# Opening loads in smaller parts and in order of use, first norm weights as columns, and a pinned sequence of the opening work in a two-layer decoder trunk

## The chip, the cores and the metric

The kernel runs on one core of a Trainium2 chip. The metric is the time of one execution on the device, in microseconds (us). The engines are TensorE (PE; PEld are its weight loads), VectorE (DVE), ScalarE (ACT), GpSimd (POOL) and SyncE (SP), which here only issues DMAs.

## The reference

Two layers over 256 tokens with 2048 features. Layer 0 mixes tokens with a chunkwise mLSTM, layer 1 with a gated linear recurrence (RG-LRU); each mixer and each SwiGLU feed-forward stands behind an RMS norm and adds to the residual. Only the start of layer 0 bears on the change:

```python
def rms_norm(x, g):
    xf = x.astype(jnp.float32)
    y = xf * lax.rsqrt(jnp.mean(xf * xf, axis=-1, keepdims=True) + EPS)
    return (y * g.astype(jnp.float32)).astype(x.dtype)
...
for layer in range(DEPTH):
    hn = rms_norm(h, norm_mix[layer])
    mix = mlstm_mixer(hn, ...)      # proj = hn @ w_in; q, k, v, o, gates = split(proj); ...
    h = h + mix
    h = h + swiglu(rms_norm(h, norm_ffn[layer]), ffn_w_in[layer], ffn_w_out[layer])
return rms_norm(h, norm_final)
```

## The kernel before

Every matrix product is done in three passes: an operand is split into a high part (a float32r rounding, the cast on ScalarE) and a low part (what is left, a subtraction on VectorE), and the products high by high, high by low and low by high are added up in PSUM.

The weights stream through four rotating buffers. `stream` loads two K tiles (256 rows of 512 columns, 512 KB, named raw0, raw2, ... by the first K tile) with one DMA of the sync queue, ScalarE makes whi (`nc.scalar.copy`, L210) and VectorE wlo (`nc.vector.tensor_tensor`, L211). `linear_feat` uses them: for each of 16 K tiles 12 matmuls of 256 columns (`mm_feat`, L309 to L311: whi by x high, whi by x low, wlo by x high, for four groups of 128 features). The first such product is qk00, the queries of the first four heads; qk01, qk10 and qk11 follow.

Its other operand is x transposed and scaled by the norm's weights, also as high and low parts. `Norm.quarter(q)` makes four K tiles of it: 8 transposes on TensorE into PSUM (L359, tile tr_m), four scalings on ScalarE (L365, the high part) and four on VectorE (L369, the low part). The scale per token, 1/rms, is applied later: `Norm.stats` sums squares of x on ScalarE (L345, eight instructions in all, result scrap into junk), `finish` turns them into factors (VectorE, GpSimd) and spreads them over all partitions with the matmul bc (L403). After it 16 matmuls gp (L545) compute the mLSTM gates from x and the small weight gwx, which is loaded as gw.

x lies in the tile h. `load_x` loads it in four DMAs of 512 columns (512 KB), with the first eight K tiles of weights between them. Norm weights and other per-feature vectors are loaded as rows, up to 128 rows of 128 numbers in each of three tiles, and turned into columns with a transpose (L181, tile par) and a copy on VectorE (`par_cols`, L183). The first rows are those of norm_mix; until par_cols(0) is done, `quarter(0)` has no weights to scale with.

The sequence on each engine is that of a scheduler: it sorts by the place in the program and by what it reckons to be ready; `tc.high_priority` pulls an instruction ahead. A DMA takes one of eight completion counters in turn, and the issuing queue waits until the DMA that had the counter before has landed. Twelve matmuls (L142, tile warm) on constants run before any data are there.

Of the kernel before, what the change touches and what calls it, by code (L numbers as in the profile page):

```python
# [8 lines left out]
F32 = mybir.dt.float32  # L9
F32R = mybir.dt.float32r  # L10
AF = mybir.ActivationFunctionType
# [3 lines left out]
P = 128  # L15
# [3 lines left out]
NK = D // P  # L19
# [5 lines left out]
NB = 512  # L25
EPS = 1e-6
BIG = 1e30
AHEAD = 1000
# [14 lines left out]
def kernel(  # L43
# [38 lines left out]
    def pool_of(key):  # L82
        return pools[key][0]
# [15 lines left out]
    def misc(name):  # L99
        return turned("misc", name) if named else bank("bank", name)  # L100
# [13 lines left out]
    h = const.tile([P, NT, D], F32, name="h")  # L114
    xv = x[0].rearrange("(b p) d -> p b d", p=P)
    raw0 = {}

    def load_raw(w, c0, ncols, kg, step=2):
        raw = pool_of("w").tile([P, 2, NB], F32, tag="raw", name=f"raw{kg}")
        wv = w.rearrange("(k p) n -> p k n", p=P)  # L120
        for i in range(0, 2, step):
            nc.sync.dma_start(raw[:, i:i + step, 0:ncols], wv[:, kg + i:kg + i + step, c0:c0 + ncols])
        return raw

    def load_x():
        for q in range(4):
            nc.sync.dma_start(h[:, :, q * NB:(q + 1) * NB], xv[:, :, q * NB:(q + 1) * NB])
# [13 lines left out]
    for i in range(12):  # L141
# [17 lines left out]
        ("gb", r_gate_b.rearrange("l g (k p) -> (l g k) p", p=P), 32),  # L159
        ("cw", r_conv_w.rearrange("l j (k p) -> (l j k) p", p=P), 64),  # L160
    ]
    par = {}
    rows = [const.tile([P, P], F32, name=f"rows{i}") for i in range(3)]
    cols = [const.tile([P, P], F32, name=f"cols{i}") for i in range(3)]
    part, at, used = 0, 0, [0, 0, 0]
    for name, src, n in par_src:
        if part == 0 and at or at + n > P:
            part, at = part + 1, 0
        nc.sync.dma_start(rows[part][at:at + n, :], src)
        if part == 0:  # L170
            load_x()
        par[name] = cols[part][:, at:at + n]
        at += n
        used[part] = at
    bif = const.tile([H, 2], F32, name="bif")
    nc.sync.dma_start(bif, m_b_if[0].rearrange("(two h) -> h two", h=H))

    def par_cols(i):
        n = used[i]
        pt = misc(f"par{i}")  # L180
        nc.tensor.transpose(pt[:, 0:n], rows[i][0:n, :], ident[0:n, 0:n])  # L181
# [13 lines left out]
    def stream(w, c0, nk, ncols=NB):  # L195

        if named:
            yield from stream4(w, c0, nk)
            return
        wpool = pool_of("w")  # L200
        for kg in range(0, nk, 2):
            first = kg in raw0
            raw = raw0.pop(kg) if first else load_raw(w, c0, ncols, kg)
            hi = wpool.tile([P, 2, NB], F32R, tag="whi", name=f"whi{kg}")
            lo = wpool.tile([P, 2, NB], F32R, tag="wlo", name=f"wlo{kg}")
            step = 1 if first and kg == 0 else 2
            with tc.high_priority(offset=0 if first else AHEAD):
                for i in range(0, 2, step):
                    r = raw[:, i:i + step, 0:ncols]
                    nc.scalar.copy(hi[:, i:i + step, 0:ncols], r)  # L210
                    nc.vector.tensor_tensor(  # L211
                        lo[:, i:i + step, 0:ncols], r, hi[:, i:i + step, 0:ncols].bitcast(F32), op=ALU.subtract
                    )
            for i in range(2):
                yield kg + i, hi[:, i, 0:ncols], lo[:, i, 0:ncols]
# [92 lines left out]
    def mm_feat(o, hi, lo, ah, al, first_in_bank, last):  # L308
        nc.tensor.matmul(o, lhsT=hi, rhs=ah, start=first_in_bank, stop=False, skip_group_check=True)  # L309
        nc.tensor.matmul(o, lhsT=hi, rhs=al, start=False, stop=False, skip_group_check=True)  # L310
        nc.tensor.matmul(o, lhsT=lo, rhs=ah, start=False, stop=last, skip_group_check=True)  # L311

    def linear_feat(w, c0, nk, act, name, after=None):

        ps = [acc(f"{name}_{b}").rearrange("p (f t) -> p f t", f=2) for b in range(2)]
        for k, hi, lo in stream(w, c0, nk):
            ah, al = act(k)
            for f in range(4):
                fs = slice(f * P, (f + 1) * P)
                mm_feat(ps[f // 2][:, f % 2, :], hi[:, fs], lo[:, fs], ah, al,  # L320
                        k == 0 and f % 2 == 0, k == nk - 1)
            if after:
                after(k)
            elif k > 1:
                run_pending()
        return ps


    class Norm:
        lag = 0  # L330
        opening = None

        def open(self):
            if self.opening:
                self.opening()

        def __init__(self, name, gain, bcast=False):
            self.name, self.gain, self.bcast = name, gain, bcast
            self.x = []
            self.ss = small.tile([P, NT, 4], F32, tag="ss", name=f"ss_{name}")  # L340

        def stats(self, q, blocks=range(NT)):
            for b in blocks:
                junk = small.tile([P, NB], F32, tag="junk", name="junk", bufs=1)
                nc.scalar.activation(  # L345
                    junk, h[:, b, q * NB:(q + 1) * NB], AF.Square,
                    accum_out=self.ss[:, b, q:q + 1],
                )

        def quarter(self, q):  # L350
            xt = pool_of("x").tile([P, 4, 2, T], F32R, tag=f"x{q}", name=f"x{q}_{self.name}")
            hi, lo = xt[:, :, 0, :], xt[:, :, 1, :]
            self.x.append(xt)
            for j in range(2):
                pt = misc(f"tr_{self.name}{q}{j}").rearrange("p (f t) -> p f t", f=2)
                for f in range(2):
                    k = 4 * q + 2 * j + f
                    for b in range(NT):
                        nc.tensor.transpose(  # L359
                            pt[:, f, b * P:(b + 1) * P], h[:, b, k * P:(k + 1) * P], ident  # L360
                        )
                for f in range(2):
                    k = 4 * q + 2 * j + f
                    g = self.gain[:, k:k + 1]
                    nc.scalar.activation(hi[:, 2 * j + f, :], pt[:, f, :], AF.Copy, scale=g)  # L365
                for f in range(2):
                    k = 4 * q + 2 * j + f
                    g = self.gain[:, k:k + 1]
                    nc.vector.scalar_tensor_tensor(  # L369
                        out=lo[:, 2 * j + f, :], in0=pt[:, f, :], scalar=g,  # L370
                        in1=hi[:, 2 * j + f, :].bitcast(F32), op0=ALU.mult, op1=ALU.subtract,
                    )

        def parts(self, q):

# [117 lines left out]
    def split_store(dst_hi, dst_lo, src):  # L493

        nc.scalar.copy(dst_hi, src)
        nc.vector.tensor_tensor(dst_lo, src, dst_hi.bitcast(F32), op=ALU.subtract)
# [18 lines left out]


    n0 = Norm("m0", par["g_mix"][:, 0:16], bcast=True)
    n0.quarter(0)
    n1 = NormPairs("f0", par["g_ffn"][:, 0:16])

    def mlstm_mixer():
        mx = open_pool("mx", "mx", 2)
        if True:
            w = m_w_in[0]
# [3 lines left out]
            gw = mx.tile([P, NK, 2 * H], F32, name="gw", bufs=1)  # L528
            nc.sync.dma_start(gw, w.rearrange("(k p) n -> p k n", p=P)[:, :, 6144:6160])
# [12 lines left out]
            n0.finish()  # L542
            gp = misc("gp")[0:4 * H, :]
            for k in range(NK):
                nc.tensor.matmul(  # L545
                    gp, lhsT=gwx[:, k, :, :].rearrange("p s n -> p (s n)"), rhs=n0.act2(k),
                    start=(k == 0), stop=(k == NK - 1),
# [568 lines left out]
```

## Time and profile before

| | |
|---|---|
| median of 3 runs | 2103.68 us (2102.78 to 2103.95) |
| the profiled execution | 2105.72 us, its span 2103.9 us |
| mean granted TensorE clock over the span | 0.997 |
| TensorE busy | 2087.6 us, 99% of the span |
| VectorE, ScalarE busy | 1673.3 us (80%), 1313.5 us (62%) |
| HBM read | 401.84 MB, 192 GB/s over the span |
| first matmul of qk00 / end of the last gp | 10.66 us / 43.34 us |

The span runs from the first to the last instruction of the profiled execution; times in the profile count from its start. Names in the profile lose their numbers: tr_m is each of the transposes' PSUM tiles, x_m the scaled x, raw, whi and wlo the weight buffers, qk the sums of the first products. "Idle" in brackets is how long an engine stood before an instruction, and behind it what released it.

### The profile page before, as it was taken

To read this page: it belongs to the slowest core of one execution; us is meant where nothing else is said; L and a number is where in the kernel's file an instruction comes from. 1 tells how busy PE (TensorE), PEld (TensorE's weight loads), DVE (VectorE), ACT (ScalarE), POOL (GpSimd) and SP (SyncE) were. 2 spreads that over 40 slices of the span, in tenths; PEclk is the share of its full clock that TensorE was granted. 3 is DMA by queue.
4 is the path that set the end of the run, shared out by engine and by line. 5 is a ranking of instruction groups with operands and counts; after the bars stand their busy time and mean duration, and the time that the engine had idled before them with its cause. 6 is when DMAs were issued, how large, how long until landed. Compare 5 with 4: busy or idle time off the path is not lost.

```text
span 2103.9 us, 27554 instructions
## 1 busy us (share of the span) xinstructions
PE 2087.6 (99%) x10544; PEld 1766.2 (84%) x10544; DVE 1673.3 (80%) x1808; ACT 1313.5 (62%) x1580; POOL 43.2 (2%) x62
## 2 busy tenths in 40 slices
PE   9999999999999999999999999999999999999998
PEld 8988888877888888888889999788888888888886
DVE  6655556699898988998876786869988898898985
ACT  5444445556676666677664758645666666666764
POOL 0001110000000000000000000000000000000002
PEclk9999999999999999999999999999999999999999
DMA  7555656556665566566555666655666565566653
GB/s 215 163 168 172 180 180 223 187 183 215 202 211 181 197 205 206 201 215 197 168 181 159 192 191 188 223 190 180 211 207 222 182 200 199 182 219 219 201 170 130
DMA packets 211085, 405.75 MB, mean 193 GB/s; under 512 B 14520, under 2 KB 14728, under 8 KB 210824
## 3 DMA queue, kind: packets, MB, share of 16 engines
q1 hardware_dynamic: 210808, 402.94, 59.6%
q8 instruction: 82, 1.34, 0.3%
q10 hardware_dynamic: 144, 1.05, 0.1%
q14 instruction: 51, 0.42, 0.1%
HBM read 401.84 MB, written 2.10 MB: 192 GB/s over the span
## 4 chain that ended last, share of the span: by engine, by line
PE 96%; ACT 2%; DVE 1%; issue 1%; DMA 0%; SPq 0%; ACTq 0%; POOLq 0%; POOL 0%; DVEq 0%
PE P L753 8%; PE P L754 8%; PE P L755 8%; PE out L753 8%; PE out L754 7%; PE out L755 7%; PE Q L753 6%; PE Q L754 6%; PE Q L755 6%; PE po L293 2%; PE po L292 2%; PE po L294 2%; PE qk L309 1%; PE qk L310 1%; PE qk L311 1%; PE v L292 1%
## 5 line engine op out<-in xcount | busy, mean ns | idle before, releaser
L211 DVE TENSOR_TENSOR wlo<-raw,whi 128x1024 fp32r<-128x1024 f32 (+1 forms) x225 | 273.1, 1218 | 183.6 <-ACT whi L210 182.5
L210 ACT CAST whi<-raw 128x1024 fp32r<-128x1024 f32 (+1 forms) x225 | 234.6, 1047 | 206.2 <-PE po L294 44.1
L236 DVE TENSOR_TENSOR wlot<-sum,whit 128x1024 fp32r<-128x1024 f32 x208 | 249.3, 1219 | 72.0 <-ACT whit L235 72.0
L753 PE MATMUL out<-whio,hh 128*128 128x512 f32 x704 | 274.9, 391 | 0.3 <-ACT out L856 0.3
L754 PE MATMUL out<-wloo,hh 128*128 128x512 f32 x704 | 274.4, 390 | 0.4 <-DVE wloo L236 0.4
L755 PE MATMUL out<-whio,hh 128*128 128x512 f32 x704 | 274.0, 390 | 0.0
L235 ACT CAST whit<-sum 128x1024 fp32r<-128x1024 f32 x208 | 213.7, 1051 | 93.7 <-PE Q L755 30.1
L235 ACT CAST whio<-rawo 128x1024 fp32r<-128x1024 f32 (+1 forms) x166 | 183.4, 1106 | 106.8 <-PE out L755 93.8
L236 DVE TENSOR_TENSOR wloo<-rawo,whio 128x1024 fp32r<-128x1024 f32 (+1 forms) x166 | 212.5, 1284 | 11.2 <-ACT whio L235 10.0
L863 ACT COPY h<-out 128x512 f32<-128x512 f32 x154 | 90.2, 586 | 186.4 <-PE out L755 186.3
L236 DVE TENSOR_TENSOR wlox<-raw,whix 128x1536 fp32r<-128x1536 f32 x104 | 182.4, 1754 | 22.4 <-ACT whix L235 22.1
L236 DVE TENSOR_TENSOR wlo<-raw,whi 128x2048 fp32r<-128x2048 f32 x72 | 164.2, 2287 | 23.4 <-ACT whi L235 23.3
L235 ACT CAST whi<-raw 128x2048 fp32r<-128x2048 f32 x72 | 137.0, 1915 | 40.5 <-DMA raw<-in_ffn_w_in_dram 26.2
L235 ACT CAST whix<-raw 128x1536 fp32r<-128x1536 f32 x104 | 154.2, 1483 | 10.6 <-PE P L755 7.6
L753 PEld LDWEIGHTS out<-whio,hh 128*128 128x128 f32 x704 | 132.2, 188 | 29.2 <-ACT out L856 1.4
L754 PEld LDWEIGHTS out<-wloo,hh 128*128 128x128 f32 x704 | 132.2, 188 | 28.5 <-DVE wloo L236 1.2
L755 PEld LDWEIGHTS out<-whio,hh 128*128 128x128 f32 x704 | 132.2, 188 | 27.8
L276 DVE TENSOR_TENSOR sum<-raw 128x1024 f32<-128x1024 f32 x104 | 127.1, 1222 | 5.0 <-DMA raw<-in_ffn_w_in_dram 3.0
L755 PE MATMUL P<-whi,p_f 128*128 128x512 f32 x282 | 110.0, 390 | 0.0
L753 PE MATMUL Q<-whi,p_f 128*128 128x512 f32 x276 | 109.7, 398 | 0.2 <-DVE h L485 0.2
L753 PE MATMUL P<-whi,p_f 128*128 128x512 f32 x282 | 109.7, 389 | 0.0
L754 PE MATMUL P<-wlo,p_f 128*128 128x512 f32 x282 | 109.7, 389 | 0.0
(284 smaller groups left out, 4995.2 us busy)
## 6 DMA issues: line engine op xcount, KB each, us to landing
raw<-in_ffn_w_in_dram SPq DMA_DIRECT2D x352, 512.0 KB, 4.7
rawo<-in_ffn_w_out_dram SPq DMA_DIRECT2D x176, 512.0 KB, 4.3
raw<-in_m_w_in_dram SPq DMA_DIRECT2D x95, 512.0 KB, 3.8
raw<-in_r_w_in_dram SPq DMA_DIRECT2D x64, 512.0 KB, 3.9
raw<-in_m_w_out_dram SPq DMA_DIRECT2D x32, 512.0 KB, 4.0
raw<-in_r_w_out_dram SPq DMA_DIRECT2D x32, 512.0 KB, 3.7
gr<-in_r_gate_w_dram SPq DMA_DIRECT2D x8, 512.0 KB, 3.8
h<-in_x_dram SPq DMA_DIRECT2D x4, 512.0 KB, 7.4
```

The costliest lines, as they stand in the source:

```text
L210: nc.scalar.copy(hi[:, i:i + step, 0:ncols], r)
L211: nc.vector.tensor_tensor(lo[:, i:i + step, 0:ncols], r, hi[:, i:i + step, 0:ncols].bitcast(F32), op=ALU.subtract)
L235: nc.scalar.copy(hi, src)
L236: nc.vector.tensor_tensor(lo, src, hi.bitcast(F32), op=ALU.subtract)
L276: nc.vector.tensor_tensor(t[:, 0:2, :], raw[:, 1:3, :], raw[:, 3:4, :].broadcast_to([P, 2, NB]), op=ALU.add)
L292: nc.tensor.matmul(o, lhsT=ah[:, bs], rhs=hi, start=(k == 0), stop=False)
L293: nc.tensor.matmul(o, lhsT=ah[:, bs], rhs=lo, start=False, stop=False)
L294: nc.tensor.matmul(o, lhsT=al[:, bs], rhs=hi, start=False, stop=(k == nk - 1))
L753: nc.tensor.matmul(o, lhsT=a[0], rhs=b[0], start=start, stop=False, **kw)
L754: nc.tensor.matmul(o, lhsT=a[0], rhs=b[1], start=False, stop=False, **kw)
L755: nc.tensor.matmul(o, lhsT=a[1], rhs=b[0], start=False, stop=stop, **kw)
L863: nc.scalar.copy(hs, o)
```

## The change

`load_x` issues x in parts of 2, 2, 4, 4 and 4 K tiles (256, 256 and three times 512 KB) and the weights of K tiles 0 to 3 in four parts of 256 KB, in the sequence of their use. The first four columns of norm weights come by a DMA of their own, issued by ScalarE, straight as columns (`gain0`: 128 partitions by 4 numbers, 4 bytes at a time), and scale quarter 0; the rows of norm_mix are issued by ScalarE as well, behind its table load. `after(...)` adds edges that pin instructions behind others on the same engine: the first weight casts behind the scalings of x, quarters 1, 2 and 3 of x behind K tiles 1, 5 and 9 (before: program places behind 3, 7 and 11, which the scheduler moved), the rows' transposes, the gate weights' split and the sums of squares further back. Sums of squares write their scrap into the PSUM bank of a transpose that is done.

```diff
@@ load_x
     def load_x():
-        for q in range(4):
-            nc.sync.dma_start(h[:, :, q * NB:(q + 1) * NB], xv[:, :, q * NB:(q + 1) * NB])
-            if q < 2:
-                for kg in (4 * q, 4 * q + 2):
-                    raw0[kg] = load_raw(m_w_in[0], 0, NB, kg, 1 if kg == 0 else 2)
+        wv = m_w_in[0].rearrange("(k p) n -> p k n", p=P)
+        for kg in (0, 2, 4, 6):
+            raw0[kg] = pool_of("w").tile([P, 2, NB], F32, tag="raw", name=f"raw{kg}")
+        def rows_of(kg, n):
+            for i in range(0, 2, n):
+                nc.sync.dma_start(raw0[kg][:, i:i + n, :], wv[:, kg + i:kg + i + n, 0:NB])
+        def features(a, b):
+            nc.sync.dma_start(h[:, :, a * P:b * P], xv[:, :, a * P:b * P])
+        features(0, 2)
+        rows_of(0, 1)
+        features(2, 4)
+        rows_of(2, 1)
+        features(4, 8)
+        rows_of(4, 2)
+        rows_of(6, 2)
+        features(8, 12)
+        features(12, 16)
...
+    gain0 = const.tile([P, 4], F32, name="gain0")
+    nc.scalar.dma_start(gain0, norm_mix[0].rearrange("(k p) -> p k", p=P)[:, 0:4])
+    load_x()
...
-        nc.sync.dma_start(rows[part][at:at + n, :], src)
-        if part == 0:
-            load_x()
+        (nc.sync if part else nc.scalar).dma_start(rows[part][at:at + n, :], src)
...
+    def after(*instructions):
+        order = ExitStack()
+        for ins in instructions:
+            order.enter_context(tc.issue_after(ins.ins))
+        return order
...
-    par_cols(0)
...
@@ stream
-            step = 1 if first and kg == 0 else 2
-            with tc.high_priority(offset=0 if first else AHEAD):
+            step = 1 if first and kg < 4 else 2
+            with after(*(n0.made[min(kg // 2, 1)][1:] if first else ())), tc.high_priority(offset=0 if first else AHEAD):
...
@@ class Norm, stats
-                junk = small.tile([P, NB], F32, tag="junk", name="junk", bufs=1)
+                junk = self.scrap
+                if junk is None:
+                    junk = small.tile([P, NB], F32, tag="junk", name="junk", bufs=1)
...
@@ class Norm, quarter (keeps the last instruction of each engine per PSUM tile)
+                self.made.append((bank_of, on_pe, on_act, on_dve))
...
-    n0.quarter(0)
+    n0.quarter(0, gain0)
+    n0.scrap = n0.made[1][0]
+    with after(*n0.made[1][1:]):
+        par_cols(0)
...
@@ mlstm_mixer
-            split_store(gwx[:, :, 0, :], gwx[:, :, 1, :], gw)
...
-            ps_q0 = linear_feat(
-                w, 0, NK, n0.act, "qk00", lambda k: n0.quarter(k // 4 + 1) if k % 4 == 3 and k < NK - 1 else None
-            )
-            par_cols(1)
-            par_cols(2)
+            def next_quarter(k, on_pe):
+                if k % 4 == 1 and k < NK - 4:
+                    with after(on_pe):
+                        n0.quarter(k // 4 + 1)
+            ps_q0 = linear_feat(w, 0, NK, n0.act, "qk00", next_quarter)
+            with after(*n0.made[7][1:]):
+                par_cols(1)
+                par_cols(2)
+                split_store(gwx[:, :, 0, :], gwx[:, :, 1, :], gw)
             for q in range(4):
-                n0.stats(q)
+                with after(n0.made[min(2 * q + 3, 7)][2]):
+                    n0.stats(q)
```

Where the instructions stand now, at three places. First the sync queue from the start of the program, before (rows are the norm weights, h is x, raw0 to raw6 the weights of K tiles 0 to 7):

```order
L169 DMA rows0_103<-in_norm_mix_dram 32x128
L127 DMA h_73<-in_x_dram 128x2x512
L122 DMA raw0_111<-in_m_w_in_dram 128x512 x2
L122 DMA raw2_114<-in_m_w_in_dram 128x2x512
L127 DMA h_73<-in_x_dram 128x2x512
L122 DMA raw4_117<-in_m_w_in_dram 128x2x512
```

and now:

```order
L136 DMA h_73<-in_x_dram 128x2x256
L133 DMA raw0_105<-in_m_w_in_dram 128x512 x2
L136 DMA h_73<-in_x_dram 128x2x256
L133 DMA raw2_106<-in_m_w_in_dram 128x512 x2
L136 DMA h_73<-in_x_dram 128x2x512
L133 DMA raw4_107<-in_m_w_in_dram 128x2x512
```

The norm rows are gone from the head of the queue, and the first 512 KB of x stand in two halves around raw0. What follows raw4 and raw6 (the rest of x, the other rows, gw, raw8) has kept its sequence.

Second TensorE behind the warm-up matmuls, before (par0 turns the norm rows, tr_m0 are the transposes of x, the digits the quarter and its half):

```order
L181 MATMUL par0_131<-ident_74,rows0_103 128x32
L359 MATMUL tr_m000_136<-ident_74,h_73 128x128 x4
L359 MATMUL tr_m001_145<-ident_74,h_73 128x128 x4
L309 MATMUL qk00_0_167<-x0_m0_135,whi0_169 128x256
L309 MATMUL qk00_1_168<-x0_m0_135,whi0_169 128x256
L359 MATMUL tr_m010_228<-ident_74,h_73 128x128 x4
L359 MATMUL tr_m011_237<-ident_74,h_73 128x128 x4
L310 MATMUL qk00_0_167<-x0_m0_135,whi0_169 128x256
```

and now:

```order
L389 MATMUL tr_m000_137<-ident_74,h_73 128x128 x4
L389 MATMUL tr_m001_146<-ident_74,h_73 128x128 x4
L206 MATMUL par0_155<-ident_74,rows0_120 128x32
L333 MATMUL qk00_0_169<-x0_m0_136,whi0_171 128x256
L334 MATMUL qk00_0_169<-x0_m0_136,whi0_171 128x256
L333 MATMUL qk00_1_170<-x0_m0_136,whi0_171 128x256
L334 MATMUL qk00_1_170<-x0_m0_136,whi0_171 128x256
L335 MATMUL qk00_0_169<-x0_m0_136,wlo0_172 128x256
```

par0 has gone behind the first transposes, and those of quarter 1 (tr_m010, tr_m011) from between the first matmuls to behind the 24 of K tiles 0 and 1. Those of quarter 2 and 3 stood together before K tile 8; now they stand before K tiles 6 and 10, and bc and all 16 gp behind K tile 15.

Third VectorE around raw8 (x2 is quarter 2 of x, cols1 and cols2 turned rows), before:

```order
L401 TENSOR_SCALAR dg_m0_487<-ident_74,rstd_m0_485 128x128 x2
L496 TENSOR_TENSOR gwx_162<-gw_160,gwx_162 128x16x16
L211 TENSOR_TENSOR wlo8_324<-raw8_321,whi8_323 128x1024
L369 SCALAR_TENSOR_TENSOR x2_m0_302<-tr_m020_303,cols0_106,x2_m0_302 128x256
L183 COPY cols1_107<-par1_460 128x112
L211 TENSOR_TENSOR wlo10_354<-raw10_351,whi10_353 128x1024
L183 COPY cols2_108<-par2_463 128x64
L369 SCALAR_TENSOR_TENSOR x2_m0_302<-tr_m020_303,cols0_106,x2_m0_302 128x256
```

and now:

```order
L399 SCALAR_TENSOR_TENSOR x1_m0_201<-tr_m011_211,cols0_123,x1_m0_201 128x256 x2
L235 TENSOR_TENSOR wlo8_328<-raw8_325,whi8_327 128x1024
L399 SCALAR_TENSOR_TENSOR x2_m0_278<-tr_m020_279,cols0_123,x2_m0_278 128x256 x2
L235 TENSOR_TENSOR wlo10_377<-raw10_374,whi10_376 128x1024
L399 SCALAR_TENSOR_TENSOR x2_m0_278<-tr_m021_288,cols0_123,x2_m0_278 128x256
L235 TENSOR_TENSOR wlo12_407<-raw12_404,whi12_406 128x1024
L399 SCALAR_TENSOR_TENSOR x2_m0_278<-tr_m021_288,cols0_123,x2_m0_278 128x256
L235 TENSOR_TENSOR wlo14_437<-raw14_434,whi14_436 128x1024
```

x2 has stayed behind wlo8 there, and on ScalarE behind whi8; the factors for bc (dg) and the gate weights have moved behind x3, after wlo of the next product's first K tiles. Behind gp the sequence of every engine is as before.

More of the change, by code (lines that the diff above doesn't have):

```diff
@@ L310, in mm_feat, with linear_feat @@
         nc.tensor.matmul(o, lhsT=hi, rhs=al, start=False, stop=False, skip_group_check=True)
-        nc.tensor.matmul(o, lhsT=lo, rhs=ah, start=False, stop=last, skip_group_check=True)
-    def linear_feat(w, c0, nk, act, name, after=None):
+        return nc.tensor.matmul(o, lhsT=lo, rhs=ah, start=False, stop=last, skip_group_check=True)
+    def linear_feat(w, c0, nk, act, name, then=None):
         ps = [acc(f"{name}_{b}").rearrange("p (f t) -> p f t", f=2) for b in range(2)]
@@ L319, in linear_feat @@
                 fs = slice(f * P, (f + 1) * P)
[L320 to L323, printed above, removed]
+                on_pe = mm_feat(ps[f // 2][:, f % 2, :], hi[:, fs], lo[:, fs], ah, al,
+                                k == 0 and f % 2 == 0, k == nk - 1)
+            if then:
+                then(k, on_pe)
             elif k > 1:
@@ L331 @@
         opening = None
+        scrap = None
         def open(self):
@@ L337, in __init__ @@
         def __init__(self, name, gain, bcast=False):
-            self.name, self.gain, self.bcast = name, gain, bcast
+            self.name, self.gain, self.bcast, self.made = name, gain, bcast, []
             self.x = []
@@ L348, in stats, with quarter @@
                 )
-        def quarter(self, q):
+        def quarter(self, q, gain=None):
+            gain = self.gain if gain is None else gain
             xt = pool_of("x").tile([P, 4, 2, T], F32R, tag=f"x{q}", name=f"x{q}_{self.name}")
@@ L358, in quarter @@
                     for b in range(NT):
-                        nc.tensor.transpose(
+                        on_pe = nc.tensor.transpose(
                             pt[:, f, b * P:(b + 1) * P], h[:, b, k * P:(k + 1) * P], ident
@@ L363, in quarter @@
                     k = 4 * q + 2 * j + f
[L364 to L365 removed]
+                    g = gain[:, k:k + 1]
+                    on_act = nc.scalar.activation(hi[:, 2 * j + f, :], pt[:, f, :], AF.Copy, scale=g)
                 for f in range(2):
                     k = 4 * q + 2 * j + f
[L368 to L369 removed]
+                    g = gain[:, k:k + 1]
+                    on_dve = nc.vector.scalar_tensor_tensor(
                         out=lo[:, 2 * j + f, :], in0=pt[:, f, :], scalar=g,
```

3 lines of the change are left out of this document (2 added, 1 removed).

## The prediction

> **What bounds the kernel now.** I read the page first: span, engines, the chain that ended last.
>
> ```profile
> span 2103.9 us, 27554 instructions
> PE 2087.6 (99%) x10544; PEld 1766.2 (84%) x10544; DVE 1673.3 (80%) x1808; ACT 1313.5 (62%) x1580; POOL 43.2 (2%) x62
> ...
> PE 96%; ACT 2%; DVE 1%; issue 1%; DMA 0%; SPq 0%; ACTq 0%; POOLq 0%; POOL 0%; DVEq 0%
> ```
>
> TensorE carries 96% of the chain. A change that touches the opening alone can only move the moment from which TensorE runs without a gap; what follows shifts with it. So the timeline of TensorE over the first 14 us comes next.
>
> ```profile
> 1.05 5.43 PE L142 MATMUL warm<-ones 128*128 128x128 f32 x24 [1.05 <-DVE mhalf L144]
> 6.41 0.25 PE L181 MATMUL par<-ident,rows 32*128 32x32 f32 x1
> 6.58 1.09 PE L359 MATMUL tr_m<-ident,h 128*128 128x128 f32 x8
> 10.66 0.80 PE L309 MATMUL qk<-x_m,whi 128*128 128x256 f32 x2 [2.98 <-ACT x_m L365]
> 11.25 1.91 PE L359 MATMUL tr_m<-ident,h 128*128 128x128 f32 x8
> 12.81 0.56 PE L310 MATMUL qk<-x_m,whi 128*128 128x256 f32 x1
> ```
>
> One hole, 2.98 us up to 10.66. The second loss is the clock, in half-microsecond windows (columns: window, length, then busy time of PE, PEld, DVE, ACT, POOL, then granted clock, DMA share, GB/s).
>
> ```profile
> 9.00:9.50 0.50, 0.00 (x0) 0.00 (x0) 0.24 (x2) 0.31 (x1) 0.00 (x0) 1.00 1.03 397
> 9.50:10.00 0.50, 0.00 (x0) 0.00 (x0) 0.00 (x0) 0.50 (x1) 0.00 (x0) 0.70 1.04 397
> 16.00:16.50 0.50, 0.50 (x4) 0.50 (x4) 0.50 (x2) 0.50 (x2) 0.00 (x0) 0.50 0.00 0
> 16.50:17.00 0.50, 0.50 (x6) 0.50 (x5) 0.50 (x1) 0.47 (x2) 0.00 (x0) 0.98 0.00 0
> ```
>
> It falls to half a little after 9.5 and is back at about 16.4, so the work from 10.66 to 16.4 costs 5.7/2 = 2.85 us extra. The chain in order of time gives the price of each TensorE step and the end of the changed stretch.
>
> ```profile
> 11.46 1.71 PE tr_m L359 x8
> 13.38 0.21 PE qk L311
> 17.67 0.12 PE qk L309
> 18.73 0.12 PE qk L309
> 25.80 1.20 PE tr_m L359 x11
> 27.85 0.30 PE par L181 x2
> 29.76 0.43 PE bc_m L403 x2
> 30.19 0.23 PE gp L545
> 40.34 3.00 PE gp L545 x13
> ```
>
> Nine matmuls lie between the two L309 rows: 1.06/9 = 0.118 us each, 0.21 at half clock. A transpose is 1.20/11 = 0.11 us (0.21 at half). The last gp ends at 40.34 + 3.00 = **43.34**. From there on both programs issue the same instructions in the same sequence on every engine, so my sum is the time of that point. Check: 192 qk matmuls 22.65, 24 transposes 2.64, par 0.30, bc 0.43, 16 gp 3.7, clock 2.85 make 32.6, and 10.66 + 32.6 = 43.3: nothing else waits in it. At most 2.98 + 2.85 = 5.8 us (0.28%) can be won.
>
> **Step 1, the smaller first loads.** The sync queue shows when bytes arrive: a DMA takes one of eight completion counters in turn and waits until the DMA eight places earlier has landed, so the norm and bias rows mark landings.
>
> ```profile
> 0.74 0.39 SPq L169 DMA_DIRECT2D rows<-in_norm_mix_dram  x1
> 1.19 0.41 SPq L127 DMA_DIRECT2D h<-in_x_dram  x1
> 7.16 0.33 SPq L169 DMA_DIRECT2D rows<-in_norm_ffn_dram  x1
> 7.79 0.33 SPq L169 DMA_DIRECT2D rows<-in_m_head_norm_dram  x1
> 16.00 0.40 SPq L529 DMA_DIRECT2D gw<-in_m_w_in_dram  x1
> ```
>
> The head-norm row waited for the second half of raw0: 16 + 512 + 2x256 = 1040 KB had landed at 7.79. In the changed sequence TensorE needs x parts 0-2 and 2-4 before anything else, and 2-4 stands behind raw0, so it too needs 256 + 512 + 256 = 1024 KB: the byte count hardly changes. What changes is the start, 0.74 instead of 1.19: landing at 7.79 - 0.45 = 7.34. Then four transposes (0.55 with their end), and on ScalarE the second pair of x and the first weight cast:
>
> ```profile
> 7.16 1.25 ACT L210 CAST whi<-raw 128x512 fp32r<-128x512 f32 x2 [0.36 <-DMA raw<-in_m_w_in_dram]
> 10.14 1.56 ACT L365 ACTIVATE x_m<-tr_m,cols 128x256 fp32r<-128x256 f32 x4
> ```
>
> 2 x 0.39 + 0.62 + handovers 0.1: first qk matmul at 9.4, against 10.66, and no transposes behind it: **1.25 us**. Bounds: 8.7 if the part lands before the warm-up matmuls end at 6.48, 10.4 if the small parts arrive a microsecond later.
>
> **Step 2, the column load of norm weights.** 512 pieces of 4 bytes. The nearest row is gw, 2048 pieces of 64 bytes:
>
> ```profile
> gw<-in_m_w_in_dram SPq DMA_DIRECT2D x1, 128.0 KB, 3.2
> raw<-in_m_w_in_dram SPq DMA_DIRECT2D x95, 512.0 KB, 3.8
> ```
>
> Issued at 0.74 it lands at 3.9 at the latest by that row, at once at the earliest; ScalarE wants it at about 7, and the third x part, which waits for its counter, is not issued before 0.74 + 6 x 0.45 = 3.4, with 1.5 MB still queued. Cost nothing, cover 3 us. The Trainium skill, "DMA: Bandwidth & Descriptors", section "Rules for kernel authors", speaks against such a load: a strided last dimension becomes one descriptor per element, and it should be rearranged. By that rule the load costs more than its 2 KB; by the gw row that is still off the path, so the sum is the same unless it takes 6 us. The two ScalarE DMAs (0.4 each) and the row-to-column transpose behind them lie in ScalarE's and TensorE's idle time before 9.4.
>
> **Step 3, the clock.** From 6.1 to 9.5 TensorE is busy about 1.6 us either way (warm-up end, par, eight transposes), so I let the clock fall at 9.5 again. The two edges lie 6.8 us apart and the stretch 10.66 to 12.9 was busy without a rise; taking stretches of 3.4 us, one that is full from 9.5 on brings the clock back at 12.9: cost 3.4/2 = 1.7, **gain 1.1**. Bounds: 0 (back at 16.4) and 2.85 (never falls). The Trainium skill, "TensorE: Matmul & The Clock Gate", section "Why this matters for your kernels", says that only idle gaps over about 3 us bring the half clock; here it fell in a hole of 2.98 us, with 1.5 us of work in the 3.4 us before, so the trace is harsher than the rule. By the rule the new hole of 1.3 us costs no clock at all.
>
> Steps 1 and 3 alone: 43.34 - 1.25 - 1.1 = 41.0.
>
> **Step 4, what is late next.** K tiles 8 and 9 (raw8); rows from the timeline by engine, in order of time, one from the chain.
>
> ```profile
> 15.81 0.64 ACT L345 ACTIVATE junk<-h 128x512 f32<-128x512 f32 x1
> 16.52 13.27 SPq L122 DMA_DIRECT2D raw<-in_m_w_in_dram  x6
> 16.57 0.64 ACT L345 ACTIVATE junk<-h 128x512 f32<-128x512 f32 x1
> 20.23 0.39 ACT L495 CAST gwx<-gw 128x256 fp32r<-128x256 f32 x1
> 23.22 1.05 ACT L210 CAST whi<-raw 128x1024 fp32r<-128x1024 f32 x1 [2.60 <-DMA raw<-in_m_w_in_dram]
> 24.30 1.23 DVE L211 TENSOR_TENSOR wlo<-raw,whi 128x1024 fp32r<-128x1024 f32 x1 [1.93 <-ACT whi L210]
> 27.00 0.31 PE qk L309 x2
> 30.97 0.48 DVE L369 SCALAR_TENSOR_TENSOR x_m<-tr_m,cols,x_m 128x256 fp32r<-128x256 f32 x1
> ```
>
> The sync queue issued raw8 at 16.52 and ScalarE waited for it until 23.2. That cost nothing, as TensorE came to it at 27. Its place on the sync queue is unchanged: behind gw, which waits for the last x part (16.00). All of that moves only by the 0.45 us of the earlier start: raw8 at 22.75. Now pinned behind it on ScalarE and VectorE are the x2 products: cast to 23.8, wlo to 25.1, low part of x2 to 25.6. TensorE, by steps 1 and 3, asks at 41.0 - 16.5 = 24.5 and stands for 1.1 us. From 25.6: 95 matmuls 11.2, eight transposes 0.9, par 0.3, bc 0.43, gp 3.7 make 42.1; and VectorE, full from there (five wlo of 1.2 and the x products of 0.48), delivers K tile 12 about 0.4 late: **42.5**. The sums of squares (0.76 apart, rows 15.81 and 16.57), then done by 20.2, are now spread between the casts; the eighth ends near 37 and bc's factors are there near 38.3, just ahead of bc at 38.5: no further wait, margin 0.2.
>
> **Sum.** 43.34 - 42.5 = 0.8 us faster. The profiled execution took 2105.72 (span 2103.9), 2.04 above the median of 2103.68; in its terms 2104.9, against the median 2103.68 - 0.8 = **2102.9**. That is 0.04%; 0.2% (4.2 us) is about what a measurement of this kernel can tell from no change.
>
> **Rivals.**
> - Raw8 comes early and binds nothing. For: the same loads usually land 3.8 us after issue (row above), here 6.6 after 16.52; against: it stands behind gw's small pieces in both kernels. Then the end is 41.0, or 40.1 where the clock also stays up: 2.3 to 3.2 us faster, 2100.5 to 2101.4.
> - Slower: the clock falls in the new wait. Before K tile 8 TensorE stands 1.1 us, 2.6 if step 3 costs no clock, inside one 3.4 us stretch; the row above shows a fall with under half a stretch busy. One stretch at half clock costs 1.7, two 3.4: 44.2 or 45.9, that is 2104.5 to 2106.2. It decides from a wait of about 1.9 us, so when raw8 lands 0.8 later or TensorE arrives 0.8 earlier than I have it. Against: the usual sum leaves two thirds of the stretch busy. The Trainium skill's rule of step 3 (idle over about 3 us) would rule this rival out.
> - The change doesn't do what it says: the second x part lands no earlier than raw0 did, in smaller runs and beside the column load (the 10.4 bound of step 1). TensorE would still be held at K tile 8: 43.2 to 43.5, so 2103.6 to 2103.9.
>
> **How the numbers follow.** My case 0.62 (gain 0.3 to 1.6: raw8 0.8 earlier or 0.5 later than I take it), raw8 early 0.18, clock falls 0.13, nothing arrives earlier 0.07. The range from 2100.8 to 2104.8 leaves out a part of the first two rivals' far ends. Beyond 4.2 us faster would need three quarters of the 5.8 us, and even raw8 on time leaves 3.2: 0.04. Beyond 4.2 slower would need two fallen stretches and raw8 late by 1.5 more: 0.04. Within: 0.92.
>
> **What would show it.** Right: first qk matmul near 9.4; no transposes between the first qk matmuls; clock up again near 13; TensorE waiting about 1 us before the first matmuls with whi8, released by VectorE's x product or ScalarE; last gp near 42.5; the rest as before. Wrong: whi8 cast before 22 (first rival), a second stretch of clock 0.5 between 23 and 30 (second), first qk matmul after 10.3 (third), or any wait in the stages after 43, which nothing here predicts.

## The result and the profile after

The changed kernel takes 2133.02 us (median of 4 runs, 2131.74 to 2133.61), the kernel before beside it 2103.81: a ratio of 1.0139 (95% interval 1.0127 to 1.0151), 1.4% slower where 0.04% faster was forecast. The profiled execution took 2133.11.

First the page of the changed kernel: the same three lines as before, and three of its costliest groups.

```profile
span 2131.3 us, 27564 instructions
PE 2117.7 (99%) x10544; PEld 1770.3 (83%) x10544; DVE 1675.7 (79%) x1809; ACT 1315.3 (62%) x1581; POOL 43.2 (2%) x62
...
PE 97%; DVE 1%; ACT 1%; issue 0%; ACTq 0%; POOLq 0%; POOL 0%; DVEq 0%
...
L794 PE MATMUL out<-whio,hh 128*128 128x512 f32 x704 | 275.8, 392 | 0.1
L794 PE MATMUL Q<-whi,p_f 128*128 128x512 f32 x276 | 111.2, 403 | 0.2
L794 PE MATMUL P<-whi,p_f 128*128 128x512 f32 x282 | 111.4, 395 | 0.0
```

The same groups on the page before (the last column is idle time ahead of them):

```profile
L753 PE MATMUL out<-whio,hh 128*128 128x512 f32 x704 | 274.9, 391 | 0.3 <-ACT out L856 0.3
L753 PE MATMUL Q<-whi,p_f 128*128 128x512 f32 x276 | 109.7, 398 | 0.2 <-DVE h L485 0.2
L753 PE MATMUL P<-whi,p_f 128*128 128x512 f32 x282 | 109.7, 389 | 0.0
```

Both kernels have 10544 matmuls, and TensorE is busy 30.1 us longer over them. There is no new wait: the idle columns stay at 0.0 to 0.3, and the waits of TensorE behind 43 us have shrunk from 2.9 us in all to one row (waits: us in all, times, the longest):

```profile
PE po L317 <- DVE wlo L235: 0.7, 2, 0.5
```

Single matmuls last longer, and not all of them: P 395 ns instead of 389 and Q 403 instead of 398, out 392 instead of 391. (These durations overlap with those of the neighbours; from one start to the next it is about 230 ns.)

The opening, which the prediction was about, went as forecast or better. The timeline of TensorE, the clock in half-microsecond windows, the cast of raw8 on ScalarE and the end of the chain up to gp:

```profile
5.70 0.85 PE L158 MATMUL warm<-ones 128*128 128x128 f32 x3
6.33 1.29 PE L389 MATMUL tr_m<-ident,h 128*128 128x128 f32 x8
7.55 0.24 PE L206 MATMUL par<-ident,rows 32*128 32x32 f32 x1
9.22 0.39 PE L333 MATMUL qk<-x_m,whi 128*128 128x256 f32 x1 [1.43 <-ACT whi L234]
```

```profile
9.50:10.00 0.50, 0.47 (x4) 0.26 (x3) 0.50 (x3) 0.50 (x2) 0.00 (x0) 0.99 1.03 389
10.00:10.50 0.50, 0.12 (x1) 0.12 (x1) 0.50 (x2) 0.50 (x2) 0.00 (x0) 0.50 1.04 389
13.00:13.50 0.50, 0.50 (x5) 0.50 (x5) 0.45 (x1) 0.50 (x1) 0.00 (x0) 0.60 1.04 385
13.50:14.00 0.50, 0.50 (x7) 0.50 (x6) 0.41 (x1) 0.06 (x1) 0.00 (x0) 1.00 1.04 376
```

```profile
22.35 1.05 ACT L234 CAST whi<-raw 128x1024 fp32r<-128x1024 f32 x1 [4.58 <-DMA raw<-in_m_w_in_dram]
```

```profile
37.80 0.63 PE bc_m L434 x2
38.43 3.66 PE gp L586 x16
```

The first qk matmul is at 9.22 (10.66 before), the clock is down from 10.0 to 13.4, and the last gp ends at 38.43 + 3.66 = 42.09 (43.34 before). The opening won 1.25 us. From that point to the end of the span, before takes 2103.9 - 43.34 = 2060.6 us and the changed kernel 2131.3 - 42.09 = 2089.2: 28.6 more, in a stretch where both issue the same instructions in the same sequence. One row of it for each, before first (columns as in the prediction's windows):

```profile
500.00:1000.00 500.00, 499.61 (x2230) 411.95 (x2229) 443.64 (x416) 339.50 (x375) 0.00 (x0) 1.00 0.61 202
```

```profile
500.00:1000.00 500.00, 500.00 (x2194) 405.39 (x2194) 437.46 (x411) 334.12 (x372) 0.00 (x0) 1.00 0.60 197
```

TensorE is full in both, the clock granted is 1.00 in both, and yet 2194 matmuls pass instead of 2230: one in 227.9 ns instead of 224.2.

To see which, I took the start of every matmul from the traces and summed the time from each start to the next by output tile (us; 512 or 256 is the number of columns):

```
tile              count   before    after   noshift  left256    x192
P       512        2112    485.9    496.2    484.7    485.8    484.6
Q       512        1800    411.4    421.4    411.6    411.4    411.5
out     512        2111    482.3    483.6    483.8    481.8    481.7
po      512         768    178.1    177.5    178.3    178.1    177.3
v, o    512         768    178.9    182.0    178.9    178.9    177.3
rec, gb 256        1536    176.0    181.0    176.0    176.0    184.4
qk      256         768     93.6     94.5     91.9     93.1     94.6
```

(The last three columns are kernels of the next section.) P and Q lose 20.3 us, rec and gb 5.0, v and o 3.1; out and po lose next to nothing. So what distinguishes P and Q from out? Not their shape, engine, clock or waits. It is where their operands lie. The byte addresses that the tiles have in each partition:

```
tile                          side    before    after
mask (constants)              left     33984    33984
gain0 (constants, 16 bytes)   left         -    34496
whi of P                      left    100640   100672
whio of out                   left     76064    76096
p0_f0 (x of P, stationary)    right   174880   174880
x0_m0 (x of v, stationary)    right   196576   196576
```

gain0 is a new tile of 16 bytes in the first pool of the left side, rounded up to 32. Every left-side tile behind it moved up by 32 bytes; the right side, counted from the top, stayed. P, Q, v, o, qk, rec and gb multiply a left tile by a right one; out and po two left ones. In before, the addresses of P's moving and stationary operands are a multiple of 256 bytes apart (174880 - 100640 = 290 x 256); in after, 32 bytes off that. From here on, distance is the address of the moving operand less that of the stationary one, as its remainder mod 256: 0 and 32 here.

### The profile page after: what moved, and what is told of

Its sections match the earlier page's. It is cut to its first block, busy times and chain, and to the rows that moved or that the text cites. A ratio compares the mean times of both kernels' runs of the same rounds, so it can differ in the third digit from the quotient of the medians.

```text
span 2131.3 us, 27564 instructions
## 1 busy us (share of the span) xinstructions
PE 2117.7 (99%) x10544; PEld 1770.3 (83%) x10544; DVE 1675.7 (79%) x1809; ACT 1315.3 (62%) x1581; POOL 43.2 (2%) x62
## 4 chain that ended last, share of the span: by engine, by line
PE 97%; DVE 1%; ACT 1%; issue 0%; ACTq 0%; POOLq 0%; POOL 0%; DVEq 0%
PE P L794 8%; PE P L796 8%; PE P L795 8%; PE out L794 8%; PE out L796 8%; PE out L795 7%; PE Q L794 7%; PE Q L795 7%; PE Q L796 6%; PE po L317 2%; PE po L318 2%; PE po L316 2%; PE qk L335 1%; PE qk L333 1%; PE qk L334 1%; PE rec L333 1%
```

## The experiments

**Where the change's tile lies (noshift).** The column goes into the constant tile mhalf, which had room up to its 32 bytes. Instructions and sequence stay.

```diff
-    mhalf = const.tile([P, 2], F32, name="mhalf")
-    nc.vector.memset(mhalf, -0.5)
+    mhalf = const.tile([P, 8], F32, name="mhalf")
+    nc.vector.memset(mhalf[:, 0:2], -0.5)
...
-    gain0 = const.tile([P, 4], F32, name="gain0")
+    gain0 = mhalf[:, 2:6]
```

> The changed kernel, with the four columns of norm weights kept in unused bytes of the tile mhalf instead of a tile of their own. In the changed kernel the new tile moved every left-side SBUF tile behind it up by 32 bytes; here none moves. Address theory: the 512-column matmuls go back from 234 to 227 ns apart and the time to about 2102.6 us (before minus the 1.25 us by which the last gp ended earlier). Sequence theory (the new order of transfers and instructions slows later stages): stays near 2133.

Measured: 2101.56 us, ratio 0.9988 (0.9979 to 0.9997). P and Q are back at 484.7 and 411.6 in the table. So the 1.4% were the address alone, and the change without it is 0.12% faster than before. From the end of gp (40.30, row further below) to the end of its span of 2100.3 are 2060.0 us, 2060.6 in before.

**The same shift without the change (left32, right32).** The kernel before, once with mhalf wider by 32 bytes (left side up), once with a 32-byte pool ahead of the right side's first (right side down). Nothing else.

```diff
-    mhalf = const.tile([P, 2], F32, name="mhalf")
+    mhalf = const.tile([P, 10], F32, name="mhalf")
```

> The kernel before, with the tile mhalf 32 bytes larger, so that all left-side tiles behind it move up by 32 bytes; nothing else changes. Address theory: about 2133 us (2103.8 plus 29), matmuls with tile P and v at 232 to 235 ns. Sequence theory: 2103.8.

```diff
+    padr = open_pool("padr", "padr", side="right").tile([P, 8], F32, name="padr")
+    nc.gpsimd.memset(padr, 0.0)
     open_pool("x", "x_m0", side="right")
```

> The kernel before, with a 32-byte tile ahead of the pools on the right side of SBUF: x and the feed-forward's left operands move down by 32 bytes, the weights stay. Relative theory (a matmul is slower where its two operands lie 32 bytes off a multiple of 64 apart): about 2133 us, slower with tiles P, Q and v, not with out and po. Absolute theory (slower where the weights' tile begins on a multiple of 64 bytes): 2103.8. Sequence theory: 2103.8.

Measured: left32 2134.48 (1.0145, 1.0131 to 1.0159), right32 2135.48 (1.0149, 1.0135 to 1.0163). Left32 shows the changed kernel's loss without any of the change:

```profile
500.00:1000.00 500.00, 500.00 (x2194) 405.06 (x2194) 437.18 (x412) 334.15 (x371) 0.00 (x0) 1.00 0.58 197
```

Moving the other side, in the other sense, does the same: it isn't the address of the weights or of x, but the distance between them.

**The shift taken back on the other side (after_right32).** The changed kernel with right32's pad: left up by 32, right down by 32.

> The changed kernel, with the same 32-byte tile ahead of the right side: weights stay 32 bytes up, x and the feed-forward's left operands go 32 down, so that the distance between the two is again a multiple of 64. Relative theory: about 2102.6 us, P at 227 ns. Absolute theory: 2133. Sequence theory: 2133.

Measured: 2119.72 (1.0073, 1.006 to 1.0085), half of the loss. That refutes a period of 64 bytes, and left open whether the period is longer or the theory is wrong. The next kernels ask that.

**The pair of reads by itself (pairs).** Ahead of the kernel before, TensorE does groups of 64 matmuls of 128x512 on one constant tile, the stationary operand at byte a and the moving one at byte b mod 256 of it.

```diff
+            for i in range(n):
+                a, b = 256 * (i % 2) + oa, 640 + 768 * (i // 2 % 2) + ob
+                nc.tensor.matmul(o, lhsT=z[:, a:a + P], rhs=z[:, b:b + NB], start=(i == 0), stop=(i == n - 1))
```

> The kernel before with a stage of its own put ahead of its first load: TensorE alone does groups of 64 matmuls of 128x512 on one constant tile, the stationary operand at byte a and the moving operand at byte b of it (mod 128, gNaMb in the names), first with no other engine at work, then four groups (busy) with VectorE and ScalarE at work on other tiles. The rest of the kernel is unchanged and comes about 400 us later. Theory 1 (the two reads of TensorE disturb each other, by the distance between their addresses): 64 matmuls take 14.5 us (227 ns each) at distance 0 and 128 mod 128, 14.9 to 15.0 (234) at distance 32 and 96, 14.6 to 14.8 (229 to 231) at 64, the same for the four groups with a = 32 when a and b are shifted alike. Theory 2 (the disturbance is between TensorE and the other engines' reads and writes): all groups with TensorE alone take 14.5, and only the busy ones differ. Theory 3 (one operand's own address counts): the time goes with a alone or with b alone.

The execution took 2508.94 us, some 400 of them in the new stage; its time is not compared. By groups (duration min/median/max in ns, then the first and the last start; a and b are in the names):

```profile
L125 PE MATMUL g0a0b<-z x64: 389/389/389, 22.7 to 37.0; 128*128 128x512 f32 x64
L125 PE MATMUL g0a32b<-z x64: 393/396/399, 37.2 to 52.0; 128*128 128x512 f32 x64
L125 PE MATMUL g0a64b<-z x64: 388/392/398, 52.2 to 66.6; 128*128 128x512 f32 x64
L125 PE MATMUL g0a96b<-z x64: 392/394/399, 66.8 to 81.5; 128*128 128x512 f32 x64
L125 PE MATMUL g0a128b<-z x64: 390/395/398, 81.8 to 96.5; 128*128 128x512 f32 x64
...
L125 PE MATMUL g0a256b<-z x64: 389/389/398, 141.6 to 155.9; 128*128 128x512 f32 x64
L125 PE MATMUL g32a0b<-z x64: 392/395/397, 156.1 to 170.8; 128*128 128x512 f32 x64
L125 PE MATMUL g32a32b<-z x64: 389/389/395, 171.0 to 185.3; 128*128 128x512 f32 x64
L125 PE MATMUL g32a64b<-z x64: 393/396/399, 185.5 to 200.2; 128*128 128x512 f32 x64
L125 PE MATMUL g32a96b<-z x64: 388/392/398, 200.5 to 214.9; 128*128 128x512 f32 x64
...
L125 PE MATMUL g0a32busy<-z x64: 393/396/399, 348.4 to 363.1; 128*128 128x512 f32 x64
```

The window from 156.1 to 333.6 shows what else went on (VectorE, ScalarE and GpSimd at 0.00, DMA share 0.00):

```profile
156.10:333.60 177.50, 177.50 (x768) 143.97 (x767) 0.00 (x0) 0.00 (x0) 0.00 (x0) 1.00 0.00 1
```

From one group's first start to the next's, 64 matmuls take 14.5 us at distance 0 (22.7 to 37.2), 15.0 at 32, 14.6 at 64, 15.0 at 96. Group g32a32b takes 14.5 again and g32a64b 15.0: only the difference b - a counts. By the starts, averaged over the last 60 of each group, in ns from matmul to matmul:

```
b - a mod 256      0     32     64     96    128    160    192    224
with a = 0     226.7  233.3  228.9  233.4  233.3  234.2  233.3  233.3
with a > 0     226.7  233.3  228.9      -      -  234.3  233.4  233.3
```

At 256 it is 226.8, as at 0. With VectorE and ScalarE at work (busy) the four groups give 227.1, 233.3, 229.0 and 233.4. So in this stage TensorE slows itself: the rate goes with the distance between the two addresses that it reads, and VectorE and ScalarE at work add at most 0.4 ns. The expectation's guess of a period of 128 was wrong.

**More distances in the kernel (left64, left96, left128, left256).** The kernel before with mhalf wider by so many bytes.

> The kernel before with 64 bytes of padding in its constant pool: all left-side tiles 64 bytes higher, the right-side ones where they were. Distance theory with a period of 64 bytes: 2104, as before, P at 227 ns from matmul to matmul. With a period of 128 bytes and half the loss at 64: 2119 to 2120, P at 226 to 231, as in the run with both sides moved by 32 in opposite senses.

> 96 bytes of padding, otherwise the same. Both periods, 64 and 128, say the same here: 2133 to 2136, P at 234. If instead the loss grows with the distance, beyond 2136; if it is the padding's parity in units of 64 on the left side alone, also 2134.

> 128 bytes of padding: same addresses mod 128 as before on both sides. Both periods say 2102 to 2105, P at 227. If any move of the left side costs, or if the period is longer than 128: over 2110.

> The kernel before with 256 bytes of padding in the constant pool: every distance between a left-side and a right-side tile the same mod 256 as before. The pair measurement (fast at distance 0 and 256, 229 at 64, 233 to 234 at the other multiples of 32) says 2102 to 2106, P at 227. If any move of the left side costs, or if the period is longer than 256: 2120 or more.

Measured, beside the runs above (P and Q: the time of both from the table's working, by 3912 matmuls):

```
kernel          distance of P, Q   time us   ratio (95% interval)       ns per P, Q
before                   0          2103.4 to 2104.1                        229.4
noshift                  0          2101.6    0.9988 (0.9979 to 0.9997)     229.1
left256                256          2103.5    1.0003 (0.9994 to 1.0012)     229.3
after_right32           64          2119.7    1.0073 (1.006 to 1.0085)      230.8
left64                  64          2121.4    1.0083 (1.0068 to 1.0098)     230.8
after                   32          2133.0    1.0139 (1.0127 to 1.0151)     234.6
left32, right32         32          2134.5, 2135.5                          234.5
left128                128          2132.7    1.0137 (1.012 to 1.0154)      234.3
left96                  96          2144.8    1.0197 (1.0181 to 1.0212)     234.6
```

Left64 and after_right32 have the same distance by different addresses and agree, but for the opening's gain that the second one has; left128 is slow, against both periods that I had; left256 restores the time. The period is 256 bytes, in the kernel as in the pair measurement. Left96 was expected at 2133 to 2136. P and Q are at 234.6 as expected, but the time is 10 us more than left32's: out takes 4.7 us longer there, rec and gb 3.6, qk 1.4. One of out's three passes, in before and then in left96 (minimum, median and maximum duration as above; L753 also goes from 389 to 393, L755 stays at 389):

```profile
L754 PE MATMUL out<-wloo,hh x704: 387/389/501, 471.1 to 2093.9; 128*128 128x512 f32 x176
```

```profile
L754 PE MATMUL out<-wloo,hh x704: 387/393/499, 476.4 to 2132.9; 128*128 128x512 f32 x176
```

Both operands of out moved by 96 bytes, so their distance is 0 in both kernels. The distance of a matmul's own operands is thus not the whole rule in the kernel; what slows out there, no run here shows.

**A better distance for v and o (x192).** In before, v and o stand at distance 64. This is noshift with 192 bytes of padding above the mixers' x tiles, which brings v and o to 0, and qk, rec and gb, where x is the moving operand, from 192 to 0.

```diff
-    open_pool("x", "x_m0", side="right")
+    def open_x(name):
+        nc.gpsimd.memset(open_pool("xpad", f"pad_{name}", side="right").tile([P, 48], F32, name="xpad"), 0.0)
+        open_pool("x", name, side="right")
+
+    open_x("x_m0")
```

> The changed kernel with the new column inside an existing tile (nothing shifted), and in addition 192 bytes of padding behind the x tiles of the two mixers on the right side, so that the matmuls of v and o too have their operands at distance 0 mod 256 instead of 64, and those of qk, rec and gb (256 columns) at 0 instead of 192. The pair measurement gives 2.2 ns less for each of the 768 matmuls of v and o: 1.7 us. If the 256-column matmuls lose in proportion too, 3.3 ns for each of 2304: 7.6 more. So 2099.9 (only 512 columns) or 2092 (both), beside 2101.6 for the version without the padding; 2101.6 if the distance does nothing in these stages because they wait for something else.

Measured: 2109.08 (1.003, 1.0018 to 1.0041), 5.7 us above the kernel before beside it. Noshift was 2.5 below its own, and 1.7 or 9 less than noshift was expected. By groups, noshift first:

```profile
L317 PE MATMUL v<-wlo,x_m x128: 388/394/481, 114.0 to 283.0; 128*128 128x512 f32 x128
L334 PE MATMUL rec<-x_m,whi x256: 276/276/283, 1101.5 to 1246.3; 128*128 128x256 f32 x128
```

```profile
L321 PE MATMUL v<-wlo,x_m x128: 387/389/481, 116.7 to 284.3; 128*128 128x512 f32 x128
L338 PE MATMUL rec<-x_m,whi x256: 280/283/283, 1100.4 to 1251.0; 128*128 128x256 f32 x128
```

v and o did go to the fast rate (394 to 389; 178.9 to 177.3 us in the table, where 1.7 less was expected), but rec and gb went from 276 to 283, 8.4 us. For these products of 256 columns distance 0 is slow and 192 fast. By the starts, a matmul of rec and gb takes 114.6 ns at 192 (before), 117.8 to 118.1 at 160 (after, left32, right32), 118.8 at 128 (left64), 120.1 at 96 (left96), 117.9 at 64 (left128) and 120.1 at 0 (x192). So one good distance doesn't serve all matmuls. That it would was a hidden assumption of mine, and the run that was to be the best version refuted it. Whether the number of columns decides, or that here the weights are the stationary operand, no run separates.

**What the opening's parts did (whole, fill).** Noshift with the first loads whole again (x parts 0 to 4, then the two halves of raw0, then raw2), and x192 with five matmuls in the hole ahead of the first qk matmul.

```diff
-        features(0, 2)
+        features(0, 4)
         rows_of(0, 1)
-        features(2, 4)
-        rows_of(2, 1)
+        rows_of(2, 2)
```

> The changed kernel with nothing shifted, but with the first loads whole again: x parts 0 to 4 in one DMA first, then the two halves of raw0, then raw2 in one; all the rest of the change stays. If the smaller parts bring the first matmul forward: first qk at about 10.2 (10.66 less the 0.45 of the earlier start), clock down in a hole of about 2.5 us, time 2102.5 to 2104. If it is the earlier start, the weight columns and the pinned sequence: first qk near 9.2, and 2101.6 as with the small parts.

Measured: 2102.21 (0.9993, 0.9984 to 1.0002); the intervals of this and noshift overlap, so the time alone doesn't tell them apart. The traces do. Noshift, timeline of TensorE:

```profile
7.00 0.66 PE L389 MATMUL tr_m<-ident,h 128*128 128x128 f32 x4 [0.54 <-DMA h<-in_x_dram]
9.10 0.38 PE L333 MATMUL qk<-x_m,whi 128*128 128x256 f32 x1 [1.26 <-ACT whi L234]
23.58 0.38 PE L334 MATMUL qk<-x_m,whi 128*128 128x256 f32 x1 [0.77 <-DVE x_m L399]
```

Whole, timeline of TensorE, and a window with its clock:

```profile
8.12 0.38 PE L332 MATMUL qk<-x_m,whi 128*128 128x256 f32 x1 [0.89 <-ACT whi L233]
23.05 0.38 PE L332 MATMUL qk<-x_m,whi 128*128 128x256 f32 x1 [0.78 <-ACT x_m L394]
24.33 0.39 PE L333 MATMUL qk<-x_m,whi 128*128 128x256 f32 x1 [0.90 <-DVE x_m L398]
```

```profile
24.00:28.00 4.00, 3.67 (x18) 3.67 (x19) 4.00 (x7) 4.00 (x9) 0.00 (x0) 0.59 0.87 223
```

With whole loads the first qk matmul comes at 8.12, earlier than either expectation (10.2 or 9.2) and 1.0 us earlier than in noshift (in all five traces with the small parts it lies between 9.05 and 9.29). The part 2 to 4 no longer stands behind raw0, and TensorE doesn't wait for it (0.54 in noshift). But TensorE then stands twice at K tile 8, 0.78 for the high part of x and 0.90 for the low, where noshift stands once. The clock falls there (0.59 on the mean from 24 to 28, 1.00 in noshift), and the last gp ends later than in noshift. From the chains, noshift and then whole:

```profile
36.59 3.71 PE gp L586 x16
```

```profile
38.82 3.71 PE gp L585 x16
```

Noshift ends gp at 40.30, whole at 42.53. Both are one execution each. That of whole took 2104.09, where the median of its eleven is 2102.21, so its late gp is probably not the usual one.

```diff
+        for i in range(5):
+            nc.tensor.matmul(pwarm[:, 0:P], lhsT=ones, rhs=ones, start=(i == 0), stop=(i == 4))
     n1 = NormPairs("f0", par["g_ffn"][:, 0:16])
```

> The run before last (nothing shifted, x tiles padded) with five matmuls of ones on ones (0.22 us each) put behind the opening's transposes, into the hole ahead of the first qk matmul. If the clock falls by the share of busy time in a stretch of 3.4 us, the filled hole keeps it at 1.00 in every execution: first qk unchanged near 9.2, last gp near 40.3, and 0 to 1.7 us faster than without the fill. If the fill delays the first qk, or the clock was mostly up already: the same time or up to 0.5 slower.

Measured: 2109.52, beside 2109.08 without the fill, with the same interval (1.0018 to 1.0041). The first qk matmul is at 9.05 and the clock stays at 1.00; but in the profiled execution of x192 it had stayed at 1.00 too. The fill gained nothing that shows; whether it would keep the clock up where it falls otherwise stays open.

## Why the prediction was wrong

**The step that failed** is the sentence "From there on both programs issue the same instructions in the same sequence on every engine, so my sum is the time of that point." The first half holds; the conclusion doesn't. The same matmul doesn't take the same time at another address, and the change moved the addresses of every left-side tile. More than ten thousand of the 10544 matmuls come after that point, and I priced the change at nothing for them without a row. They took 28.6 us longer; the table has 28.4 for P, Q, rec, gb, v and o. No rival covered it either: all three lay in the opening, and "slower" was forecast from two fallen clock stretches and a late load. I also named the wrong mark for it, "any wait in the stages after 43": there is no wait, the rate changed.

**Step 1** had the size (9.22 forecast as 9.4, 1.44 us earlier instead of 1.25) but not the reason. My sum took the byte count ahead of the second part of x as hardly changed, and the start 0.45 earlier as the gain. With whole loads all else of the change brings the first matmul to 8.12, in one execution. So the earlier first matmul comes from the rest: the earlier start, the weights as columns and the x products pinned ahead of the casts (these three were not tried apart). The small parts, which I counted as neutral, cost 1.0 at that point.

**Step 2**, the column load at no cost to the path: right as a load, though it took 3.7 us to land, more than my bound of 3.2. ScalarE's first scaling, at 7.10, waited for TensorE's transposes and not for it. Its price was the 32 bytes of the tile that it lands in.

**Step 3**, the clock: one stretch at half clock instead of two, from 10.0 to 13.4 instead of 9.5 to 12.9. It fell although the longest hole there was 1.43 us, against the rule from the Trainium skill that I had set beside it ("TensorE: Matmul & The Clock Gate", section "Why this matters for your kernels": no idle gaps over about 3 us between bursts of matmuls, or the clock goes back to half). In noshift, with a hole of 1.26 at the same place, it did not fall, and in whole it fell around two waits of under 1 us. The traces side with the busy time in a stretch. In each trace the clock changes at whole multiples of 3.41 us from its first clock record. That record lies elsewhere in each, with the same instructions too: at 6.28 in before, 5.19 in left32, 4.20 in left64. Three such stretches, of whole, of the changed kernel and of noshift:

```profile
21.33:24.75 3.42, 1.75 (x13) 1.35 (x12) 2.09 (x4) 3.17 (x6) 0.00 (x0) 1.00 1.03 392
6.58:9.99 3.41, 1.96 (x13) 1.33 (x11) 2.02 (x6) 2.89 (x7) 0.00 (x0) 1.00 1.05 386
5.35:8.76 3.41, 1.94 (x15) 1.43 (x14) 1.06 (x3) 1.90 (x5) 0.00 (x0) 1.00 1.05 384
```

The clock was down behind the first two and not behind the third. Over all traces but that of pairs, it was down behind every stretch at full clock with TensorE busy for 1.75 us or less, behind none with 2.10 or more, and behind some of those from 1.86 to 1.98. So where the stretches happen to begin decides, and the gain is in part one of chance: about 1.1 us in the profiled execution of the changed kernel, all of the 2.85 in that of noshift.

**Step 4**, the new wait at K tile 8: there, with 0.4 us instead of 1.1, since raw8's cast came at 22.35 and not 22.75.

```profile
25.10 0.39 PE L334 MATMUL qk<-x_m,whi 128*128 128x256 f32 x1 [0.36 <-DVE x_m L399]
```

The sum for the last gp was 42.5, measured 42.09. The rival "the clock falls in the new wait" did not happen here, but its mechanism is real: in whole, TensorE comes to K tile 8 at 22.3 instead of the forecast 24.5, waits 1.7 in all, and the clock falls there, near the 1.9 that the rival named as its point.

The account of the 27.4 us of span: P and Q +20.3, rec and gb +5.0, v and o +3.1, out +1.3, po -0.6, the end of gp -1.25: 27.9, which is 0.5 too much.

## What to carry to other kernels

A new tile, however small, may move the address of everything behind it: compare the tiles' addresses of both programs, and work out for the costliest matmuls the distance between stationary and moving operand, before you call a later stage unchanged. The trace of a tuned kernel shows whether that matters: groups of one form with different median durations and no waits (here one line of v at 394 beside P at 389) may run at different distances already. Where operands come from both ends of the memory, a pad of a few bytes is a parameter to tune, for each form of matmul by itself, and to be measured: in x192 the pad that helped v and o cost rec and gb more.

## What the hardware showed that I had not expected

TensorE alone, with no other engine and no DMA at work, does a 128x512 float32r matmul in 226.7 ns when the addresses of its two operands differ by a multiple of 256 bytes, in 228.9 at 64, and in 233.3 to 234.3 at the other multiples of 32: up to 3.4%. With 256 columns, in rec and gb, the order is another: 114.6 ns at distance 192 (before), 117.8 at 160 (after) and 120.1 at 0 (x192). And out in left96 is slower at distance 0. Why the distance matters, no run here shows.
